# Index scores in tiles of their own, first queries one gate later, three gate projections moved behind the attention's output projection

## The chip, the cores and the metric

The kernel runs on one core of one Trainium2 chip. The metric is the device time of one execution in microseconds (us), as the median of several executions. TensorE (PE), VectorE (DVE), ScalarE (ACT), GpSimd (POOL) and the DMA queues run beside each other and meet through semaphores. TensorE's clock has two levels, 1.2 and 2.4 GHz; the profile shows the granted share as 0.50 and 1.00.

## The reference, cut to what matters

The model is one hybrid block (a convolution branch and a sparse attention branch side by side, then a feed-forward layer) followed by two more layers (gated linear attention and block attention, each with a feed-forward layer). The change lies in the first block alone. There are 272 tokens (16 meta tokens and 256 of the input), 1024 channels, 8 heads of 128 with 2 key groups.

```
proj = h @ w_in                      # u_conv, q, k, v, q_idx, k_idx, w_idx, gates
y_a = conv branch(u_conv)            # a * sigmoid(gate), 31-tap depthwise convolution, layer norm, silu, @ conv_pw_out
dots  = q_idx . k_idx / 8            # 8 index heads
score = sum_h w_idx[h] * relu(dots[h]) / sqrt(8)
keep the 68 best keys of each query (the 16 meta tokens always), softmax attention over them
y_b = attention(...) @ w_o
g_a, g_b = sigmoid(gates)            # 1024 columns each
stream = stream + (g_a * y_a + g_b * y_b) @ w_merge_out
```

## The kernel before, in words

**Weights.** All large weights lie in one DRAM array in the order of their use, cut into halves of 128 x 1024 numbers; one DMA of 1024 KB on SP's queue brings two. Every half is split into two parts for TensorE: ACT copies it into `whi` (line 134), and DVE subtracts that copy from it into `wlo` (line 136). One projection of 128 output rows takes one half and 24 matmuls (8 slices of the contraction, three products each; `proj_tile`, lines 175 to 177). The splits run at most five halves ahead of the projection that stands at the same place of the program (`may_split`, `LOOK` = 5; six buffers each of `whi` and `wlo`). Halves are counted here from 0: 0 to 15 are the convolution's input, 16 to 19 the index queries, 20 and 21 the keys, 22 and 23 the values, 24 to 31 the queries, 32 to 47 the gates, 48 to 55 the attention's output projection, 56 to 63 the convolution's output projection.

**Order.** The order of the instructions on every engine is fixed when the program is built. Among the instructions whose inputs are ready by the builder's estimate, the one that stands first in the program goes first; what stands in a `high_priority` block goes ahead of all that does not. Each engine then runs its own list strictly in order.

**PSUM.** Projections write into `ps_acc` tiles, of which there are four; index scores, transposes and attention use `ps_wk` tiles, four as well. A fifth `ps_acc` projection waits until the first of the four has been read.

**The stages around the change, in the order of the program.**

- Index queries, then the two key projections. After each of them, and after each of the three value projections, a generator `index_scores` (line 467) is moved on by one piece. For each of two query tiles t and each of 8 heads it makes a matmul (line 474), a relu by ACT into a small tile `r` (line 477; its tag `s1` has two buffers and is shared with `rope`) and a multiply-add by DVE (line 478). Then DVE picks the best keys with seven rounds of `max` and `match_replace` (lines 485 and 488).
- Eight query projections, each with `rope` (lines 520 to 524).
- The loop over 8 heads (line 607). Head i has two gate projections, j = 0 for the convolution's gate g_a and j = 1 for the attention's gate g_b, each evacuated by an ACT tanh (line 611), with pieces of the previous head's attention between them. `attend` has scores (line 553), softmax on DVE and ACT (lines 534 to 539), transposes (556 to 561) and, every fourth head, the product with the values (566 to 570) that writes `oT`. `attend_first` treats the two meta queries that the output needs; its first piece (the copy at line 578 and the matmuls at line 580) stands ahead of the first gate.
- `conv()` (line 620). Its 31 taps stand here in the program, but they become ready long before: DVE and ACT take them whenever nothing that stands earlier is ready. DVE's taps are line 389; ACT's products are line 406, added by DVE at line 412 or by an accumulating DMA of POOL's queue (line 410) into `ysum`, which line 423 adds at the end.
- The convolution's layer norm and silu (lines 641 to 660), a `high_priority` block. It needs the whole convolution. DVE adds (645, 646), PE takes the mean (648), DVE subtracts it (650) and sums squares (654), PE and POOL make the reciprocal root (631, 635, 638), then come DVE (658), ACT's silu (659) and the split into `sT` (200 and 202).
- The attention's output projection (line 661): eight projections m0 to m7 over `oT`; DVE evacuates each (line 664) into the gate tile `tg[1]`.
- The convolution's output projection (line 667): eight projections over `sT`; DVE evacuates each (671) with the gate tile `tg[0]`.

Of the kernel before, what the change touches and what calls it, by code (L numbers as in the profile page):

```python
# [65 lines left out]
    FIRST += [(0, 1, 0, 3 * (_k - 5) + _i) for _i in range(3) if _k > 4 and 3 * (_k - 5) + _i < KT]  # L66
FIRST += [(1, 1, 0, _k) for _k in range(KT)]
PACE = 2
LATER = mybir.DependencyInfo(mybir.DependencyClass.NoSync, mybir.DependencyReason.DATA)
LK = 5  # L70
CONV_ACT = (((0,), (1,), 2), ((0,), (1,), 3))
# [13 lines left out]
def tile_hybrid(ctx: ExitStack, tc: tile.TileContext, x, meta, wts, misc, vec, cst, rows, gkw, ng, pos,  # L85
# [13 lines left out]
    def ps_wk():  # L99
        return wk.tile([P, 512], F32, name="ps_wk", tag="ps_wk")  # L100

    def dump(name, ap):
        if dbg and name in dbg:
            nc.sync.dma_start(dbg[name], ap)
# [320 lines left out]
    def rope(o, ps, a, b, ti, parts=()):  # L425
        n = b - a
        sw = sc.tile([P, L], F32, name="sw", tag="s1", bufs=2)[:, :n]
        t1 = sc.tile([P, L], F32, name="t1", tag="s2", bufs=3)[:, :n]
        A.activation(sw[0:64], ps[64:128], AF.Copy)
        A.activation(sw[64:128], ps[0:64], AF.Copy)  # L430
        V.tensor_mul(t1, ps, tabs[:, ti, a:b])
        V.tensor_mul(sw, sw, tabs[:, ti + 1, a:b])
        V.tensor_add(t1 if parts else o, t1, sw)
        for dst, lo in parts:
            A.activation(dst, t1[lo:lo + 32], AF.Copy)
# [31 lines left out]
    def index_scores():  # L467
        for t in range(2):
            nk = P * (t + 1)
            sco = mp.tile([P, SEQ], F32, name="sco", tag="sco", bufs=2)[:, :nk]  # L470
            vm = vmask[:, SEQ - nk:]
            for h in range(8):
                pd = ps_wk()
                PE.matmul(pd[:, :nk], qi[h // 2][:, t * P:(t + 1) * P], kidx[h % 2][:, :nk],
                          start=True, stop=True)
                r = sc.tile([P, SEQ], F32, name="r", tag="s1", bufs=2)[:, :nk]
                A.activation(r, pd[:, :nk], AF.Relu)
                V.scalar_tensor_tensor(sco, r, wix[:, t, h:h + 1], vm if h == 0 else sco,
                                       op0=OP.mult, op1=OP.add)
                if h == 3:  # L480
                    yield
            m8 = mp.tile([P, 8], F32, name="m8", tag="m8", bufs=2)
            n8 = TOP_X
            while n8 > 0:
                V.max(m8, sco)
                if n8 < 8:
                    V.memset(m8[:, n8:], -GONE)
                V.match_replace(sco, m8, sco, GONE)
                n8 -= 8
            b = mp.tile([P, L], F32, name=f"bias{t}")  # L490
            V.memset(b[:, :META], 0.0)
            V.tensor_scalar(sco, sco, -2.0e38, NEG, op0=OP.is_gt, op1=OP.mult)
            V.tensor_add(b[:, META:META + nk], sco, vm)
            bias.append(b)
            dump(f"bias{t}", b[:, :META + nk])
            yield
# [24 lines left out]
    for h in range(N_HEADS):  # L521
        pq = ps_acc()
        proj_tile(pq[:, :NQ], hT, T0, L)
        rope(qT[:, h, :], pq[:, :NQ], T0, L, 0)
    dump("qT", qT)

    oT = (mp.tile([P, KT, NQ], F32R, name="oT_h", tag="oT_h"),
# [47 lines left out]
    def attend_first():  # L575
        ps = ps_wk()[:8, :2 * META].rearrange("p (g k) -> p g k", g=2)
        q2 = mp.tile([P, 2 * N_HEADS], F32, name="q2")
        V.tensor_copy(q2.rearrange("p (h q) -> p h q", q=2), qT[:, :, 0:2])
        for g in range(2):
            PE.matmul(ps[:, g, :], q2[:, 8 * g:8 * g + 8], kT[g][:, :META], start=True, stop=True)  # L580
        l_ = mp.tile([8, 2, META], F32, name="l2")
        st = mp.tile([8, 2, 2], F32, name="st2")
        V.tensor_add(l_, ps, m2[:, None, :].to_broadcast([8, 2, META]))
        V.tensor_reduce(st[:, :, 0], l_, axis=mybir.AxisListType.X, op=OP.max)
        V.tensor_sub(l_, l_, st[:, :, 0:1].to_broadcast([8, 2, META]))
        A.activation(l_, l_, AF.Exp, scale=scale)
        V.tensor_reduce(st[:, :, 1], l_, axis=mybir.AxisListType.X, op=OP.add)
        V.reciprocal(st[:, :, 0], st[:, :, 1])
        V.tensor_mul(l_, l_, st[:, :, 0:1].to_broadcast([8, 2, META]))
        yield  # L590
        pp = ps_wk()
        for g in range(2):
            PE.transpose(pp[:META, 8 * g:8 * g + 8], l_[:, g, :], ident[:8, :8])
        pT = mp.tile([META, 16], F32, name="pT2")
        A.activation(pT, pp[:META, :16], AF.Copy)
        yield
        po = ps_wk()
        for g in range(2):
            PE.matmul(po[:, 8 * g:8 * g + 8], vt[2][:META, g * P:(g + 1) * P], pT[:, 8 * g:8 * g + 8],
                      start=True, stop=True)  # L600
        split(oT[0][:, :, 0:2], oT[1][:, :, 0:2], po[:, :16].rearrange("p (h q) -> p h q", q=2))
        yield

    tg = [mp.tile([P, KT, NQ], F32, name=f"tg{i}", tag=f"tg{i}") for i in range(2)]
    live = [attend_first()]
    next(live[0])
    for i in range(KT):
        for j in range(2):
            pg = ps_acc()
            proj_tile(pg[:, :NQ], hT, T0, L)  # L610
            A.activation(tg[j][:, i, :], pg[:, :NQ], AF.Tanh, scale=0.5)
            for a in live:
                next(a)
        live = [attend(i, t) for t in range(2)]
        for a in live:
            next(a)
    for _ in range(2):
        for a in live:
            next(a)
# [41 lines left out]
    for m in range(KT):  # L661
        py = ps_acc()
        proj_tile(py[:, :NQ], oT, 0, NQ)
        V.scalar_tensor_tensor(tg[1][:, m, :], tg[1][:, m, :], 1.0, py[:, :NQ], op0=OP.add, op1=OP.mult)

    mT = (mp.tile([P, KT, NQ], F32R, name="mT_h", tag="oT_h"), mp.tile([P, KT, NQ], F32R, name="mT_l", tag="oT_l"))
    for m in range(KT):
# [563 lines left out]
def _pack(a):  # L1231
    w = a["w_in"][0]
    c = np.cumsum([0, 2048, 1024, 256, 256, 512, 64, 8, 2048])
    u, q, k, v, qi, ki, wi, g = (w[:, c[i]:c[i + 1]] for i in range(8))
    u, g = _ws(u), _ws(g)
    qi = qi.reshape(D, 4, 2, 2, 32).transpose(0, 1, 3, 2, 4).reshape(D, 512)
    v = v.reshape(2, 4, P, 256).transpose(0, 2, 1, 3).reshape(2, P, HALF)
    pair = lambda z: z.reshape(2, 8, P, HALF).transpose(1, 0, 2, 3).reshape(16, P, HALF)
    gl = a["gla_w_in_2"][0]
    gq, gk, gv, gg, glow = np.split(gl, [512, 1024, 2048, 3072], axis=1)  # L1240
    gu, gd = a["ffn_w_gu_2"], a["ffn_w_down_2"]

    def out_ffn(o, up, down, ahead=()):
        o = o.reshape(KT, P, HALF)
        return o[:4], _first(up), o[4:], _ffn(up, down, True, ahead)

    mw = _xs(a["moba_w_in_2"][0])

    parts = [pair(u), _ws(qi), _ws(k), v, _ws(q), pair(g), _ws(a["attn_w_o"][0]), _ws(a["conv_pw_out"][0]),
             _ws(a["w_merge_out"][0]), _ffn(a["ffn_up"][0], a["ffn_down"][0], False),  # L1250
             _xs(gq), _xs(gv), _xs(gk), _xs(gg), *out_ffn(a["gla_w_out_2"][0], gu[0], gd[0], mw[:4]),
             mw[4:], *out_ffn(a["moba_w_out_2"][0], gu[1], gd[1])]
    wts = np.concatenate(parts)
    wts = np.ascontiguousarray(wts.reshape(-1, 2, P, HALF).transpose(0, 2, 1, 3)).reshape(-1, P, CHUNK)
    k1, k2 = ki[:, :32], ki[:, 32:]
    pad = np.zeros((D, 32), w.dtype)
    m = np.concatenate([k1, wi, pad[:, 8:], k2, pad, glow], axis=1)
    misc = m.reshape(KT, P, NMISC).transpose(1, 0, 2).reshape(P, KT * NMISC)
    col = lambda z: z.reshape(-1, P).T
    taps = lambda z: z.reshape(z.shape[0], -1, P).transpose(2, 1, 0).reshape(P, -1)  # L1260
    vec = np.concatenate([col(a["mix_norm_g"]), col(a["conv_ln_g"]), col(a["conv_ln_b"]), taps(a["conv_dw_w"][0]),
                          col(a["conv_dw_b"]), col(a["ffn_norm_g"]), taps(a["ffn_dw_w"][0]),
                          col(a["ffn_dw_b"])], axis=1)
    rows = [a["final_norm_g"]]
    for i in range(2):
        for j in range(2):
            rows += [a["ln_g_2"][i, j], a["ln_b_2"][i, j]]
    gkw = np.concatenate([a["gla_w_gk_2"][0], a["gla_b_gk_2"]], axis=0)
    return {"x": a["x"], "meta": a["meta_tokens"], "wts": wts, "misc": misc, "vec": vec, "cst": _constants(),
            "rows": np.stack(rows), "gkw": gkw, "ng": a["gla_norm_g_2"], "pos": a["positions_2"]}  # L1270
# [48 lines left out]
```

## Time and profile before

| | us |
|---|---|
| runs shown: median of 3 (lowest to highest) | 1074.39 (1074.29 to 1075.55) |
| the profiled execution, its own time | 1076.28 |
| its span from the first to the last instruction | 1074.5 |
| granted TensorE clock, mean of the span | 0.995 |

The profile is of one execution, which took 1.9 us more than the median of the runs shown; 1.8 us of its time lie outside its span. Busy times are unions of an engine's instructions. A matmul's end is modelled, so a busy PE is not a PE at its peak; waits are read from start times. "Idle before" names what ended an engine's idle time.

### The profile page before, as it was taken

What the parts mean: (1) busy time and instruction counts of PE and PEld (TensorE: products, weight loads), DVE (VectorE), ACT (ScalarE), POOL (GpSimd) and SP (SyncE); (2) the same over time, 40 slices, a digit from 0 to 9 for tenths busy, and PEclk for the clock granted to TensorE, in tenths of its full rate; (3) what the DMA queues carried; (4) which work ended last, traced back from release to release, by engine and by line L of the source; (5) the groups of instructions that cost most, each with busy time, mean ns of one, the idle gap of its engine ahead of it and who ended that gap; (6) DMA issues with size and microseconds to landing.
All of it is one profiled execution on the core that took longest, in us unless ns stands there. A gap on an engine that the chain in (4) does not pass through costs nothing. (4 is left out here: it accounts for less than half of the span.)

```text
span 1074.5 us, 17515 instructions
## 1 busy us (share of the span) xinstructions
PE 1054.8 (98%) x6989; PEld 954.5 (89%) x6989; DVE 739.5 (69%) x1291; ACT 601.0 (56%) x1051; POOL 44.1 (4%) x52
## 2 busy tenths in 40 slices
PE   8999999999999999999999999999999999999997
PEld 8998998899899999977877999999888878999995
DVE  6899999995776767774577655556674766555555
ACT  6897698564555555567463444446256925444440
POOL 0131002100000000000000000000000000000000
PEclk8999999999999999999999999999999999999999
DMA  8886556564354555454453655557263436555541
GB/s 307 246 201 161 191 166 178 148 220 169 142 197 160 195 182 192 174 185 139 153 202 112 236 196 179 180 191 274 79 215 138 164 131 226 187 195 194 173 144 40
DMA packets 33333, 192.37 MB, mean 179 GB/s; under 512 B 3889, under 2 KB 7857, under 8 KB 12002
## 3 DMA queue, kind: packets, MB, share of 16 engines
q1 hardware_dynamic: 28002, 185.02, 49.7%
q0 software_dynamic: 5248, 6.23, 3.6%
q8 instruction: 55, 0.90, 0.3%
q14 instruction: 28, 0.23, 0.1%
HBM read 183.96 MB, written 1.05 MB: 172 GB/s over the span
## 5 line engine op out<-in xcount | busy, mean ns | idle before, releaser
L136 DVE TENSOR_TENSOR wlo<-wraw,whi 128x1024 fp32r<-128x1024 f32 x320 | 388.5, 1223 | 204.8 <-ACT whi L134 203.9
L134 ACT ACTIVATE whi<-wraw 128x1024 fp32r<-128x1024 f32 x322 | 337.3, 1058 | 302.0 <-PE ps_wk L176 117.7
L176 PE MATMUL ps_wk<-hT_l,whi 128*128 128x256 f32 (+1 forms) x976 | 274.9, 282 | 0.0
L177 PE MATMUL ps_wk<-hT_h,wlo 128*128 128x256 f32 (+1 forms) x976 | 274.6, 281 | 0.0
L175 PE MATMUL ps_wk<-hT_h,whi 128*128 128x256 f32 (+1 forms) x976 | 274.2, 281 | 0.0
L175 PEld LDWEIGHTS ps_wk<-hT_h,whi 128*128 128x128 f32 x976 | 184.4, 189 | 1.1
L176 PEld LDWEIGHTS ps_wk<-hT_l,whi 128*128 128x128 f32 x976 | 184.0, 189 | 1.4
L177 PEld LDWEIGHTS ps_wk<-hT_h,wlo 128*128 128x128 f32 x976 | 184.8, 189 | 0.4
L181 PE MATMUL ps_acc<-whi,rg_h 128*128 128x512 f32 x328 | 131.1, 400 | 0.0
L182 PE MATMUL ps_acc<-wlo,rg_h 128*128 128x512 f32 x328 | 129.6, 395 | 0.0
L183 PE MATMUL ps_acc<-whi,rg_l 128*128 128x512 f32 x328 | 127.1, 395 | 0.0
L175 PE MATMUL ps_acc<-hT_h,whi 128*128 128x258 f32 (+2 forms) x352 | 101.9, 290 | 0.0
L177 PE MATMUL ps_acc<-hT_h,wlo 128*128 128x258 f32 (+2 forms) x352 | 100.7, 286 | 0.0
L176 PE MATMUL ps_acc<-hT_l,whi 128*128 128x258 f32 (+2 forms) x352 | 100.5, 285 | 0.0
L183 PEld LDWEIGHTS ps_acc<-whi,rg_l 128*128 128x128 f32 x328 | 61.6, 188 | 14.7 <-DVE rg_l L202 0.2
L181 PEld LDWEIGHTS ps_acc<-whi,rg_h 128*128 128x128 f32 x328 | 61.6, 188 | 14.1 <-ACT rg_h L200 0.2
L182 PEld LDWEIGHTS ps_acc<-wlo,rg_h 128*128 128x128 f32 x328 | 61.7, 188 | 12.8
L181 PE MATMUL ps_acc<-whi,hT_h 128*128 128x512 f32 (+1 forms) x184 | 71.8, 390 | 0.0
L183 PE MATMUL ps_acc<-whi,hT_l 128*128 128x512 f32 (+1 forms) x184 | 70.8, 385 | 0.0
L182 PE MATMUL ps_acc<-wlo,hT_h 128*128 128x512 f32 (+1 forms) x184 | 70.6, 384 | 0.0
L175 PEld LDWEIGHTS ps_acc<-hT_h,whi 128*128 128x128 f32 x352 | 66.2, 188 | 0.3
L176 PEld LDWEIGHTS ps_acc<-hT_l,whi 128*128 128x128 f32 x352 | 66.3, 188 | 0.2
(950 smaller groups left out, 1561.7 us busy)
## 6 DMA issues: line engine op xcount, KB each, us to landing
wraw<-in_wts_dram SPq DMA_DIRECT2D x166, 1024.0 KB, 5.0
ysum<-zs POOLq DMA_DIRECT2D x10, 258.0 KB, 6.9
x<-in_x_dram SPq DMA_DIRECT2D x4, 512.0 KB, 3.8
lg<-in_rows_dram SPq DMA_DIRECT2D x4, 512.0 KB, 3.6
lb<-in_rows_dram SPq DMA_DIRECT2D x4, 512.0 KB, 5.4
wraw<-in_wts_dram SPq DMA_DIRECT2D x2, 512.0 KB, 6.5
out_dram<-x SPq DMA_DIRECT2D x4, 256.0 KB, 2.0
mraw<-in_misc_dram SPq DMA_DIRECT2D x1, 576.0 KB, 12.3
```

What stands on the lines that cost most here:

```text
L134: A.activation(hi, r, AF.Copy)
L136: V.tensor_sub(lo, r, hi.bitcast(F32))
L175: PE.matmul(ps, wh, xh, start=first, stop=False)
L176: PE.matmul(ps, wh, xl, start=False, stop=False)
L177: PE.matmul(ps, wl, xh, start=False, stop=last)
L181: PE.matmul(ps, xh, wh, start=first, stop=False)
L182: PE.matmul(ps, xh, wl, start=False, stop=False)
L183: PE.matmul(ps, xl, wh, start=False, stop=last)
```

## The change

Index scores: the relus of a query tile go into one tile `r8` of eight heads that takes the storage of the gate tile of the same number (`tg0`, `tg1`, free at that time), instead of the two small shared buffers. One PSUM tile takes four heads (query tile 0) or two (query tile 1), and one ACT instruction evacuates it. The generator now has seven pieces instead of five, so that the query projections move it on too. `attend_first` begins behind the first gate instead of ahead of it. The gates j = 0 of heads 5, 6 and 7 leave the head loop and stand behind the attention's output projection, ahead of the convolution's; their weights move to the same place of the weight array. So the halves are now 32 to 44 for the thirteen gates that stay, 45 to 52 for the attention's output projection, 53 to 55 for the three gates that moved; 56 to 63 are what they were.

```diff
+LEFT = 3
...
-            for h in range(8):
-                pd = ps_wk()
-                PE.matmul(pd[:, :nk], qi[h // 2][:, t * P:(t + 1) * P], kidx[h % 2][:, :nk],
-                          start=True, stop=True)
-                r = sc.tile([P, SEQ], F32, name="r", tag="s1", bufs=2)[:, :nk]
-                A.activation(r, pd[:, :nk], AF.Relu)
-                V.scalar_tensor_tensor(sco, r, wix[:, t, h:h + 1], vm if h == 0 else sco,
-                                       op0=OP.mult, op1=OP.add)
-                if h == 3:
+            r8 = mp.tile([P, 8, SEQ], F32, name="r8", tag=f"tg{t}")[:, :, :nk]
+            wide = 512 // nk
+            for h0 in range(0, 8, wide):
+                if h0:
                     yield
+                pd = ps_wk().rearrange("p (a b) -> p a b", a=wide)
+                for a in range(wide):
+                    h = h0 + a
+                    PE.matmul(pd[:, a, :], qi[h // 2][:, t * P:(t + 1) * P], kidx[h % 2][:, :nk],
+                              start=True, stop=True)
+                A.activation(r8[:, h0:h0 + wide, :], pd, AF.Relu)
+                for h in range(h0, h0 + wide):
+                    V.scalar_tensor_tensor(sco, r8[:, h, :], wix[:, t, h:h + 1], vm if h == 0 else sco,
+                                           op0=OP.mult, op1=OP.add)
...
         rope(qT[:, h, :], pq[:, :NQ], T0, L, 0)
+        next(scores, None)
...
-    live = [attend_first()]
-    next(live[0])
+    def gate(j, i):
+        pg = ps_acc()
+        proj_tile(pg[:, :NQ], hT, T0, L)
+        A.activation(tg[j][:, i, :], pg[:, :NQ], AF.Tanh, scale=0.5)
+
+    first = attend_first()
+    live = [first]
     for i in range(KT):
         for j in range(2):
-            pg = ps_acc()
-            proj_tile(pg[:, :NQ], hT, T0, L)
-            A.activation(tg[j][:, i, :], pg[:, :NQ], AF.Tanh, scale=0.5)
+            if j or i < KT - LEFT:
+                gate(j, i)
             for a in live:
-                next(a)
+                next(a, None)
         live = [attend(i, t) for t in range(2)]
         for a in live:
             next(a)
+        if i == 0:
+            live.append(first)
...
         V.scalar_tensor_tensor(tg[1][:, m, :], tg[1][:, m, :], 1.0, py[:, :NQ], op0=OP.add, op1=OP.mult)
+    for i in range(KT - LEFT, KT):
+        gate(0, i)
...
+    g = pair(g)
+    left = [2 * i for i in range(KT - LEFT, KT)]
+    keep = [i for i in range(2 * KT) if i not in left]
...
-    parts = [pair(u), _ws(qi), _ws(k), v, _ws(q), pair(g), _ws(a["attn_w_o"][0]), _ws(a["conv_pw_out"][0]),
+    parts = [pair(u), _ws(qi), _ws(k), v, _ws(q), g[keep], _ws(a["attn_w_o"][0]), g[left], _ws(a["conv_pw_out"][0]),
```

## Rows read from the trace of the kernel before

**Rows 1.** The page's first part, busy time of each engine in the span.

```profile
PE 1054.8 (98%) x6989; PEld 954.5 (89%) x6989; DVE 739.5 (69%) x1291; ACT 601.0 (56%) x1051; POOL 44.1 (4%) x52
```

**Rows 2.** PE's waits: line <- releaser: us in total, times, longest us.

```profile
PE ps_wk L474 <- ACT r L477: 1.8, 2, 1.6
...
PE ps_wk L580 <- DVE q L578: 0.8, 1, 0.8
```

**Rows 3.** Stretches: length, busy us of PE, PEld, DVE, ACT, POOL; clock; DMA.

```profile
136.00:196.70 60.70, 60.59 (x434) 53.40 (x433) 59.85 (x156) 53.45 (x156) 12.62 (x13) 1.00 0.66 170
196.70:224.70 28.00, 25.75 (x207) 24.76 (x206) 25.00 (x53) 18.28 (x33) 1.80 (x1) 1.00 0.43 140
```

**Rows 4.** DVE's timeline about the convolution's end: start us, length us, instruction.

```profile
185.75 1.23 DVE L136 TENSOR_TENSOR wlo<-wraw,whi 128x1024 fp32r<-128x1024 f32 x1
186.88 0.86 DVE L389 SCALAR_TENSOR_TENSOR yc<-hp,dwh,yc 128x248 f32<-128x248 f32 x2
...
196.30 0.46 DVE L389 SCALAR_TENSOR_TENSOR yc<-hp,dwh,yc 128x242 f32<-128x242 f32 x1
...
198.59 1.23 DVE L423 TENSOR_TENSOR yc<-yc,ysum 128x1032 f32<-128x1032 f32 x1 [0.69 <-DMA ysum<-zs]
199.75 1.22 DVE L136 TENSOR_TENSOR wlo<-wraw,whi 128x1024 fp32r<-128x1024 f32 x1
```

**Rows 5.** ACT's timeline, the copy that the split at 199.75 subtracts.

```profile
186.95 1.06 ACT L134 ACTIVATE whi<-wraw 128x1024 fp32r<-128x1024 f32 x1 [0.24 <-PE ps_acc L176]
```

**Rows 6.** DVE's busy time by line 136 alone between 188 and 196.7 us.

```profile
188.00:196.70 8.70, 0.00 (x0) 1.00 0.72 135
```

**Rows 7.** DVE's timeline in the layer norm, output evacuations (L664) among it.

```profile
202.09 0.42 DVE L664 SCALAR_TENSOR_TENSOR tg<-tg,ps_acc 128x258 f32<-128x258 f32 x1
...
204.17 0.42 DVE L664 SCALAR_TENSOR_TENSOR tg<-tg,ps_acc 128x258 f32<-128x258 f32 x1
...
210.46 0.42 DVE L664 SCALAR_TENSOR_TENSOR tg<-tg,ps_acc 128x258 f32<-128x258 f32 x1
...
212.60 0.42 DVE L664 SCALAR_TENSOR_TENSOR tg<-tg,ps_acc 128x258 f32<-128x258 f32 x1
...
213.67 1.20 DVE L136 TENSOR_TENSOR wlo<-wraw,whi 128x1024 fp32r<-128x1024 f32 x1
216.29 2.76 DVE L658 TENSOR_TENSOR yc<-yc,ps_wk 128x258 f32<-128x258 f32 x8 [1.42 <-PE ps_wk L638]
218.97 0.42 DVE L664 SCALAR_TENSOR_TENSOR tg<-tg,ps_acc 128x258 f32<-128x258 f32 x1
...
221.78 0.41 DVE L664 SCALAR_TENSOR_TENSOR tg<-tg,ps_acc 128x258 f32<-128x258 f32 x1
```

**Rows 8.** PE's timeline, from the layer norm to the end of the convolution's output projection.

```profile
203.17 1.14 PE L648 MATMUL ps_wk<-sqb,ones 128*128 128x258 f32 x4 [0.40 <-DVE sqb L646]
203.96 0.47 PE L176 MATMUL ps_acc<-oT_l,whi 128*128 128x258 f32 x1
...
212.86 0.62 PE L631 MATMUL ps_wk<-ones,sqb 128*128 128x1 f32 x6
...
215.68 0.58 PE L638 MATMUL ps_wk<-cs,rs 128*128 128x128 f32 x3 [1.39 <-POOL rs L635]
...
220.12 0.28 PE L175 MATMUL ps_acc<-sT_h,whi 128*128 128x258 f32 x1
...
221.59 0.39 PE L176 MATMUL ps_acc<-sT_l,whi 128*128 128x258 f32 x1 [0.47 <-DVE sT_l L202]
...
243.84 0.28 PE L685 MATMUL ps_acc<-cs,mt_again 128*128 128x2 f32 x2
```

**Rows 9.** Stretches at the program's start and end, columns as in rows 3.

```profile
13.00:19.80 6.80, 6.67 (x27) 6.24 (x28) 6.63 (x12) 5.31 (x10) 0.00 (x0) 0.50 0.78 321
...
1066.80:1071.00 4.20, 0.00 (x0) 0.00 (x0) 4.09 (x8) 0.00 (x0) 0.92 (x1) 1.00 0.00 0
1071.10:1074.50 3.40, 0.00 (x0) 0.00 (x0) 0.20 (x1) 0.00 (x0) 0.00 (x0) 0.50 0.41 154
```

## The prediction, made before the changed kernel ran

> **What bounds the kernel now.** I began with the page's busy times: PE is busy for 98% of the span [rows 1], so a gain can come only from waits of PE, and there are few. Next came PE's waits. The index scores' matmuls wait 1.8 us for ACT's relus, the first queries' matmuls 0.8 us for DVE [rows 2]. Together 2.6 us is what the first two edits can take off PE.
>
> The third view, the stretches, says that this need not reach the end. From 136 to 196.7 us DVE is busy for 59.85 of 60.70 us [rows 3]: DVE and PE are both full there, and DVE's list ends with the convolution, for which the layer norm waits. In the next 28.0 us PE is busy for only 25.75. So the view that matters is DVE's list about 196.7 us. It shows who stands behind whom. The copy for split 53 is done at 188.0 (186.95 + 1.06) [rows 5], yet DVE subtracts it only at 199.75 [rows 4]; between 188 and 196.7 it makes no split at all [rows 6]. Split 52, which stands ahead of `conv()` in the program, came at 185.75; split 53 stands behind it. So DVE takes what stands behind `conv()` only when the taps have run out. The same holds for the evacuations of the output projection (line 664): the first runs at 202.09, and the fifth only at 218.97, behind the layer norm's eight multiplications [rows 7].
>
> **The change part by part.** All times are of the profiled execution (1076.28 us), which is 1.9 us over the median.
>
> *Index scores and first queries.* The wait at line 474 and most of that at line 580 go: up to 2.6 us of PE. DVE's sixteen multiply-adds and the matmuls stay. ACT has six wide relus in place of sixteen. The storage of `r8` is free, and is read out before the first gate writes it. If the waits stay after all, the loss is at most these 2.6 us, and what comes next hides it either way.
>
> *The convolution ends earlier.* The last gate in the head loop is now half 44, so only splits up to 49 stand ahead of `conv()`, where splits up to 52 stood. A split holds DVE for 1.13 us (185.75 to 186.88 [rows 4]). Three fewer make 3.4 us, and DVE has no idle time to lose: the last tap ends at 196.76 - 3.4 = 193.4. Bounds: 0, if something else of DVE's takes the place, and 4.1, if the wait of 0.69 us for the accumulating DMA [rows 4] goes too. I take 3.4, and the whole layer norm moves by as much.
>
> *PE runs out of work sooner.* A projection takes (243.84 - 220.12 - 0.47) / 8 = 2.9 us [rows 8], so three gates are 8.7 us. Before, m3 ended at about 220.12 less four projections (11.6) and the layer norm's pieces behind it (0.62 + 0.58 + 1.39 of wait), that is 205.9 [rows 8]. In the new order three gates less (8.7), no early waits (2.6) and no line 648 ahead of it (1.2, from 0.40 ahead of 203.17 to 203.96) bring its end to 193.4. Then m4 needs a fifth `ps_acc`: it waits for the evacuation of m0, which stands behind the convolution. That one ended at 202.51 and now ends at 199.1. PE stands idle for 5.7 us, and the 2.6 us won early are part of this wait. Split 49 is ready by then.
>
> *The gates that moved are no filler where a wait is.* PE goes on: m4, line 648 (0.8) and m5 until 205.7; m6 waits for the third evacuation (210.88 - 3.4 = 207.5); m6 and m7 with lines 631 and 638 end at about 214 to 215.9. The first gate that moved needs the buffer of m4, so the evacuation that ran at 218.97: it ends at 219.39 - 3.4 = 216.0. The second needs that of m5, 222.19 - 3.4 = 218.8, just in time. Three gates make 216.0 + 8.7 = 224.7, and only then does PE come to the convolution's output projection. Before, it began at 220.12 and lost 0.47 us more, in effect 220.6. By then the layer norm is finished, so that loss goes. **The sum is 224.7 - 220.6 = 4.1 us more**: 1080.4 on the profiled execution, 1078.5 on the median of 1074.39. From there on nothing is changed and PE is the bound, so it reaches the end.
>
> *Costed at nothing.* The tanhs of the three gates now fall among the layer norm's ACT work; ACT is busy for 18.28 of 28.0 us there [rows 3]. The weights are the same loads on SP's queue in another order. The late splits 50 and 51 give their raw buffer back at about 200, and the load that waits for it brings halves used from 224.7 on; with that cover gone it would cost its landing. The gates pass nothing on POOL's queue.
>
> *The clock.* At the start TensorE ran at the lower level, 0.50, from 13.0 to 19.8; at the end, 4.2 us without a matmul passed at 1.00, and then the rows show 0.50 [rows 9]. A wait of 5.7 us is longer than those 4.2. The Trainium skill ("TensorE: Matmul & The Clock Gate", "Why this matters for your kernels") warns of idle gaps between bursts of matmuls, which put the clock back to its lower level; it speaks against this change, and rows 9 agree. By that rule the time would be that of the third rival below rather than 1078.5.
>
> **The rivals.**
>
> *Half of it.* PE does idle until 199.1, but the builder finds gaps for the later evacuations, so that no gate waits. Then PE's work alone counts: 199.1 + 0.8 + 11.6 + 0.62 + 0.58 + 8.7 = 221.4, or 222.8 with the 1.39 at line 638: 0.8 to 2.2 us more than 220.6. For it: DVE has 3.0 us without work between 196.7 and 224.7 [rows 3]. Against it: rows 7 show one thing taken in each gap, and split 213.67 went into the longest. I price it at +1.5, 1075.9.
>
> *Faster.* The evacuations and splits fall among the taps, and PE never runs dry. The place is DVE between m3's end and the last tap; the price is the early waits (2.6) and the 0.47 at `sT_l`, 3.1 us less, 1071.3. It decides at the first evacuation: by the sum of the case above, the change is no loss if that ends before about 197 to 198. For it: taps also wait for ACT's products, and a dry spell would let evacuations in. Against it: rows 6 show 8.7 us without one, and each split among the taps gives back 1.1 of the 3.4 us.
>
> *The clock falls in the wait.* PE comes back at the lower level. For as long as in rows 9 (6.8 us) that costs half of it, 3.4 us; the wait of m6 covers 207.5 - 205.7 = 1.8, so 1.6 remain on top of 4.1: 1080.1. For it: rows 9; against it: no wait of this length lies between matmuls in the trace of before.
>
> *The change doesn't do what it says.* If line 474 still waits, 1.8 us return. In my forecast that is hidden by the wait at m4; in the faster case it leaves a gain of 1.3.
>
> **How the numbers follow.** The forecast has 0.43, the clock 0.20, half of it 0.20, faster 0.17. The forecast's own range is 1077.0 to 1081.5: a convolution that ends 4.1 earlier takes 0.7 off, one that gains 1 us less adds 1, and the part of the clock's price that isn't covered adds 1.6. The range that should hold the time 8 times in 10 is 1072.0 to 1081.5; it leaves out most of the faster case (0.12) and the upper end of the others (0.07). A measurement tells about 0.2%, 2.1 us, from no change. Slower by more: forecast and clock less a little, 0.60. Within it: half of it, and the faster case where line 474 still waits, 0.25. Faster by more: 0.15.
>
> **What would show it.** Right: no PE wait at line 474; the last tap near 193.4; DVE without evacuations until then; PE idle before m4 by some 6 us, released by DVE's line 664; the first gate that moved released by a later one near 216; the convolution's output projection from about 224.7. Wrong: evacuations among the taps, or a convolution that ends no earlier, or a PE that is busy from 190 to 216.

## The result, and the profile after

The changed kernel takes 1089.05 us (median, 1086.55 to 1090.04); the kernel before took 1074.97 beside it. The ratio is 1.0123, 95% interval 1.0107 to 1.0140: slower, as forecast, but by 13.2 us where 4.1 were forecast, and outside the range. (The 13.2 us come from the ratio, as do the differences to the kernel before further down; the two medians lie 14.1 us apart.) The profiled execution took 1089.12 us with a span of 1087.0, 12.5 more than the 1074.5 before.

The first part of the page, busy time of each engine, beside [rows 1]:

```profile
PE 1059.4 (97%) x6989; PEld 959.5 (88%) x6989; DVE 741.0 (68%) x1291; ACT 599.3 (55%) x1041; POOL 44.0 (4%) x52
```

The number of PE's instructions is the same, its busy time 4.6 us longer (1059.4 - 1054.8). The idle time is 1087.0 - 1059.4 = 27.6 us, before 1074.5 - 1054.8 = 19.7. So the loss has two parts: 7.9 us in which PE does nothing, and 4.6 us in which it does the same work more slowly. PE's waits show the first part (columns as in [rows 2]):

```profile
PE ps_acc L176 <- DVE tg L676: 6.9, 2, 4.1
PE ps_wk L586 <- DVE q L584: 3.5, 1, 3.5
```

Line 676 is the evacuation of the output projection (line 664 before), line 586 the first queries (580 before, 0.8 us). The wait at the index scores, 1.8 us before, is gone. Now PE's timeline, beside [rows 8]; lines 660, 643, 650 are 648, 631, 638 of before:

```profile
200.37 0.58 PE L176 MATMUL ps_acc<-oT_h,whi 128*128 128x258 f32 x1 [4.13 <-DVE tg L676]
200.75 0.42 PE L177 MATMUL ps_acc<-oT_l,whi 128*128 128x258 f32 x1
200.96 0.42 PE L178 MATMUL ps_acc<-oT_h,wlo 128*128 128x258 f32 x1
...
201.61 1.92 PE L660 MATMUL ps_wk<-sqb,ones 128*128 128x258 f32 x4
...
209.98 0.58 PE L176 MATMUL ps_acc<-oT_h,whi 128*128 128x258 f32 x1 [2.80 <-DVE tg L676]
...
213.34 0.62 PE L643 MATMUL ps_wk<-ones,sqb 128*128 128x1 f32 x6
...
216.16 0.58 PE L650 MATMUL ps_wk<-cs,rs 128*128 128x128 f32 x3 [1.28 <-POOL rs L647]
...
224.40 0.36 PE L176 MATMUL ps_acc<-hT_h,whi 128*128 128x258 f32 x1
...
233.10 0.28 PE L176 MATMUL ps_acc<-sT_h,whi 128*128 128x258 f32 x1
```

Counted in the trace, 96 matmuls of the output projection (m0 to m3) stand ahead of the first wait and 120 (m0 to m4) ahead of the second: the waits are at m4 and at m5. Look at two things. Behind the wait at 200.37 the matmuls start 0.21 us apart (200.75, 200.96), where at full rate it is 0.12. And line 650, the layer norm's second transpose, runs at 216.16, almost where it ran before (215.68 in [rows 8]); but now 51 matmuls of the output projection and 72 of the gates stand behind it, before 32. So the convolution's output projection starts at 233.10 instead of 220.12. The early part of the order has brought nothing, and the gates are still to be done.

The stretches show the clock (columns: length, busy us of PE, PEld, DVE, ACT, POOL, granted clock, DMA share, GB/s):

```profile
131.40:134.70 3.30, 3.30 (x18) 3.30 (x17) 3.30 (x9) 2.83 (x5) 0.00 (x0) 0.50 0.62 206
196.30:200.30 4.00, 0.00 (x0) 0.00 (x0) 3.90 (x6) 0.92 (x1) 0.00 (x0) 0.92 0.47 131
200.40:206.40 6.00, 6.00 (x24) 5.62 (x25) 4.49 (x11) 1.43 (x4) 0.00 (x0) 0.50 0.51 175
...
210.00:213.30 3.30, 3.30 (x15) 3.30 (x16) 2.07 (x4) 0.00 (x0) 0.00 (x0) 0.50 0.00 0
...
216.80:220.10 3.30, 3.30 (x16) 3.30 (x17) 3.06 (x9) 2.53 (x3) 0.00 (x0) 0.50 0.71 288
```

Four stretches have a granted clock of 0.50, the level of 1.2 GHz, each behind one of the four waits (3.46 us at the first queries, 4.13, 2.80, 1.28). In the kernel before, none of them is there. The two of 3.30 us at the layer norm hold 15 and 16 matmuls, where 27 fit at 0.12 us: some 1.4 us lost in each.

Last, DVE about the convolution's end, beside [rows 4] and [rows 7] (line 390 is the tap, 424 the sum, 662 the layer norm's subtraction):

```profile
192.68 1.23 DVE L390 SCALAR_TENSOR_TENSOR yc<-hp,dwh,yc 128x243 f32<-128x243 f32 x3
...
196.40 1.23 DVE L424 TENSOR_TENSOR yc<-yc,ysum 128x1032 f32<-128x1032 f32 x1 [1.34 <-DMA ysum<-zs]
...
199.90 0.41 DVE L676 SCALAR_TENSOR_TENSOR tg<-tg,ps_acc 128x258 f32<-128x258 f32 x1
...
203.56 1.43 DVE L662 TENSOR_TENSOR yc<-yc,ps_wk 128x258 f32<-128x258 f32 x4 [1.51 <-PE ps_wk L660]
...
209.51 0.41 DVE L676 SCALAR_TENSOR_TENSOR tg<-tg,ps_acc 128x258 f32<-128x258 f32 x1
...
214.01 0.21 DVE L645 TENSOR_SCALAR st<-ps_wk 128x2 f32<-128x2 f32 x2 [1.94 <-PE ps_wk L643]
```

The taps end at 193.91 and the first evacuation comes at 199.90. The second comes only at 209.51, behind the layer norm's subtractions; before it came ahead of them, at 204.17. Now DVE waits for PE as well, 1.51 us for the mean (line 660) and 1.94 for the variance (line 643): both stand in PE's queue behind matmuls that were waiting for DVE's evacuations. So the two engines wait for each other in turn, while a convolution that ends 2.9 us earlier (193.91 for 196.76) does not end the layer norm earlier. How much of the delay this ring makes is told in part by a run below: with the evacuations first, DVE reads the variance (line 645) at 212.81 instead of 214.01.

### The profile page after: what moved, and what is told of

Read it like the earlier page. It is cut to its first block, busy times and chain, and to the rows that moved or that the text cites. A ratio compares the mean times of both kernels' runs of the same rounds, so it can differ in the third digit from the quotient of the medians.

```text
span 1087.0 us, 17484 instructions
## 1 busy us (share of the span) xinstructions
PE 1059.4 (97%) x6989; PEld 959.5 (88%) x6989; DVE 741.0 (68%) x1291; ACT 599.3 (55%) x1041; POOL 44.0 (4%) x52
## 5 line engine op out<-in xcount | busy, mean ns | idle before, releaser
L182 PEld LDWEIGHTS ps_acc<-whi,rg_h 128*128 128x128 f32 x328 | 61.6, 188 | 14.3 <-ACT rg_h L201 0.6
```

The costliest lines, as they stand in the source:

```text
L182: PE.matmul(ps, xh, wh, start=first, stop=False)
```

## The experiments

In all of them the ratio is to the kernel before, timed on the same chip beside it.

### Which part of the change loses

No gate moved, the two other edits as in the changed kernel:

```
-LEFT = 3
+LEFT = 0
```

> The changed kernel with all sixteen gate projections back ahead of the output projection (index scores and first queries stay as changed). Theory (the loss is the three moved gates: without them TensorE runs out of free PSUM tiles while VectorE still has the convolution's taps and splits, and then works at half clock): both waits of 4.13 and 2.80 us at the output projection vanish, the half-clock spells behind them too, and what is left is the index's 1.8 us gained against the longer wait at the first queries (3.5 us for 0.8, and one half-clock spell): 1073.0 to 1077.5 us. Rival (the index tiles and the first queries carry the loss, for instance through VectorE's order): 1085 or more.

Measured: 1078.85 us, 1.0019 (1.0006 to 1.0033), 2.0 us; the median is 1.4 us above the theory's range, and far from the rival's. The two waits at the output projection are gone. The ten executions fall into two groups: three with a mean granted clock of 0.995 took 1075.47 to 1076.34 us, seven with 0.990 to 0.993 took 1078.10 to 1080.11. So most of the 2.0 us goes with the lower clock. The other way round, the kernel before with the three gates moved and nothing else:

```
-            pg = ps_acc()
-            proj_tile(pg[:, :NQ], hT, T0, L)
-            A.activation(tg[j][:, i, :], pg[:, :NQ], AF.Tanh, scale=0.5)
+            if j or i < KT - LEFT:
+                gate(j, i)
...
+    for i in range(KT - LEFT, KT):
+        gate(0, i)
```

> The kernel before with only the three gates moved; index scores and first queries as before. Theory: the two waits and the half-clock spells at the output projection are there as in the changed kernel, the index waits of 1.8 us are back, the 3.5 us wait at the first queries is back at 0.8: 1085 to 1091 us. Rival (the parts of the change only lose together, because the early gain lets TensorE arrive too soon): 1077 to 1080, two thirds of the loss gone.

Measured: 1.0112 (1.0090 to 1.0134), 12.0 us. The waits of both kernels, no gate moved first:

```profile
PE ps_wk L586 <- DVE q L584: 4.1, 1, 4.1
```

```profile
PE ps_acc L176 <- DVE tg L669: 7.9, 2, 5.1
...
PE ps_wk L475 <- ACT r L478: 2.2, 2, 1.6
```

So the gates carry the loss, with the early edits or without. What the index scores and first queries add is a loss of 2.0 us alone, not a gain; beside the gates it is about 1 us, which is not clear of the noise.

### How the loss grows with the gates

One gate moved instead of three (`LEFT = 1`):

> The changed kernel with one gate moved instead of three. Theory (each gate ahead of the output projection fills 2.9 us of wait and clock): TensorE comes 5.8 us later to m4, after the evacuation of m0, so the wait of 4.13 us goes; m5 still waits up to 3 us for that of m1; 75 matmuls stand behind the layer norm's second transpose, against 123 and 32: the convolution's output projection from 224 to 227 us, 1077 to 1082 us. Rival (a step: any moved gate costs the whole since the layer norm splits the order at one place): 1086 or more. Rival (no loss below two gates): under 1077.

Measured: 1082.52 us, 1.0063 (1.0050 to 1.0076), 6.8 us, just above the theory's range. With the 2.0 us of no gate moved, that makes 4.8 us for the first gate and (13.2 - 6.8) / 2 = 3.2 for each of the next two. A gate is 2.9 us of matmuls. The wait at m4 has gone (PE waits 1.38 us for the layer norm's sums at line 660 instead), that at m5 is 2.13 us, and the transposes run at 215.85, where 216.16 and 215.68 stood: the layer norm's end hardly moves, and each gate that is taken out of the time ahead of it is added behind it. No step is seen, and no free first gate.

### Is it the clock, or the waits?

Redundant matmuls, ahead of m3 and of m5, fill the two waits (their result is overwritten by the tile that follows):

```
+FILL = {3: 34, 5: 14}
...
         py = ps_acc()
+        for _ in range(FILL.get(m, 0)):
+            PE.matmul(py[:, :NQ], oT[1][:, KT - 1, 0:P], oT[1][:, KT - 1, :], start=True, stop=True)
         proj_tile(py[:, :NQ], oT, 0, NQ)
```

> The changed kernel with redundant matmuls put where TensorE waits: 34 ahead of the output projection's tile m3 and 14 ahead of m5, each into the tile that is overwritten next, so that the result is the same and only the idle time is filled. Theory (the clock is the greater part of the loss: 13.6 us at half clock behind the waits stretch the output projection and the layer norm's matmuls by some 6.8 us): the granted clock stays at 1.00 from 196 to 220 us and the time falls by 5 to 9 us, to 1080 to 1084. Rival (the waits alone cost, VectorE's chain sets the end, and the clock lies in its shadow): the clock stays up but the time stays within 2 us of the changed kernel's, 1087 to 1091.

Measured: 1086.51 us, 1.0101 (1.0078 to 1.0124), 2.5 us under the changed kernel's median, with intervals that overlap. The stretches of this kernel:

```profile
196.00:200.00 4.00, 4.00 (x34) 3.81 (x32) 2.36 (x3) 0.00 (x0) 0.00 (x0) 1.00 0.39 81
200.00:202.20 2.20, 0.02 (x1) 0.00 (x0) 2.20 (x6) 0.00 (x0) 0.00 (x0) 1.00 0.24 97
202.20:206.00 3.80, 3.78 (x15) 3.41 (x16) 2.75 (x6) 0.80 (x1) 0.00 (x0) 0.55 0.41 121
206.00:216.00 10.00, 8.03 (x66) 7.56 (x64) 8.16 (x19) 5.18 (x12) 1.78 (x1) 1.00 0.35 128
216.10:230.00 13.90, 13.90 (x115) 13.71 (x116) 12.88 (x26) 11.75 (x23) 0.00 (x0) 1.00 0.51 177
```

From 206 us on the clock stays at 1.00, so 210 to 213.3 and 216.8 to 220.1 are cured; one slow stretch is left, behind a wait of 2.20 us for the layer norm's mean, which is new because the last accumulating DMA landed later (the sum that waits for it began at 197.64, not at 196.40). Neither expectation held: the fall lies between them. The transposes stay at 216.06 and the convolution's output projection starts at 230.87. With the clock up behind 216, the 119 matmuls that stand there still take 14.3 us (119 x 0.12), where the kernel before has 32. So the clock is the smaller part, though this run, with its new wait and one slow stretch left, does not give its exact share.

### Two more PSUM tiles

```
-        py = ps_acc()
+        py = ps_wk() if m in (4, 5) else ps_acc()
```

> The changed kernel with the output projection's tiles m4 and m5 in two tiles of the other PSUM pool, so that they need no evacuation. Theory (the wait is for a free PSUM tile): the 4.13 us wait at m4 goes or falls under 1.5, TensorE is at m6 by 202.5, a shorter wait comes at m7 or at the first moved gate, and fewer half-clock spells are left: 1079 to 1086 us. Rival (VectorE's order is the limit, each further tile only moves the wait): within 2 us of the changed kernel, 1087 to 1091.

Measured: 1.0128 (1.0109 to 1.0148), as the changed kernel. The edit did not do what it was for. The builder put the two tiles in the other pool last:

```profile
217.02 0.58 PE L176 MATMUL ps_wk<-oT_h,whi 128*128 128x258 f32 x1
```

so PE still came to a fifth `ps_acc` first, and waited 4.14 us for the same evacuation. This says nothing for or against either theory; it says that an edit to storage is also an edit to the order.

### The evacuations first

The changed kernel, with the one line that reads PSUM put ahead of DVE's other work:

```
-        V.scalar_tensor_tensor(tg[1][:, m, :], tg[1][:, m, :], 1.0, py[:, :NQ], op0=OP.add, op1=OP.mult)
+        with tc.high_priority():
+            V.scalar_tensor_tensor(tg[1][:, m, :], tg[1][:, m, :], 1.0, py[:, :NQ], op0=OP.add, op1=OP.mult)
```

> The changed kernel with one thing more: the evacuations of the output projection come ahead of all other work of VectorE (high priority), so they run among the convolution's taps. Theory (TensorE is the bound; its two waits of 4.13 and 2.80 us for an evacuation, the half-clock spells behind them, and the work that therefore still stands behind the layer norm's wait near 216 us make the loss): no wait for an evacuation above 0.5 us, one half-clock spell or none between 196 and 222 us, 51 matmuls of 0.12 us for 123 behind the layer norm's second transpose, the convolution's output projection from 222 to 224 us: 1075 to 1079. Rival (the taps and so the layer norm come later by what the evacuations take on VectorE, and the three gates cost their 8.7 us all the same): 1082 or more.

Measured: 1078.6 us, 1.0032 (1.0021 to 1.0043). Of the loss of 13.2 us, 9.8 are gone ((1.0123 - 1.0032) x 1075), with the same three gates behind the output projection. DVE's timeline shows evacuations (line 677 here) among the taps:

```profile
190.10 0.42 DVE L677 SCALAR_TENSOR_TENSOR tg<-tg,ps_acc 128x258 f32<-128x258 f32 x1
190.44 1.23 DVE L390 SCALAR_TENSOR_TENSOR yc<-hp,dwh,yc 128x245 f32<-128x245 f32 x3
191.60 0.41 DVE L677 SCALAR_TENSOR_TENSOR tg<-tg,ps_acc 128x258 f32<-128x258 f32 x1
```

and PE's stretches show that the clock holds until 213 us:

```profile
196.00:212.90 16.90, 14.70 (x117) 14.02 (x116) 15.61 (x31) 6.60 (x12) 0.00 (x0) 1.00 0.36 106
213.00:216.00 3.00, 3.00 (x14) 2.47 (x14) 1.27 (x3) 0.00 (x0) 1.79 (x1) 0.50 1.02 352
```

No wait for an evacuation is left, 51 matmuls stand behind the transposes, which run at 214.95, and the convolution's output projection starts at 222.22, as expected. Two waits for late splits (`wlo`) are new, 0.70 us at 199.58 and 1.50 us at 211.47, ahead of the slow stretch at 213 us. The price is small: the taps end 0.7 us later (194.64 for 193.91). This is the run that settles the cause of the greater part: who stands behind whom on DVE.

The kernel before with the gates moved and the evacuations first, index scores and first queries as before:

> The kernel before with the three gates moved and the evacuations at high priority; index scores and first queries as before. Theory (the moved gates alone cost nothing if the evacuations don't stand behind the convolution): the index's waits of 1.8 us are back, the first queries' wait is 0.8 us, no half clock at 131 us: 1074 to 1077.5. Rival (the gates cost something by themselves, since 51 matmuls stand behind the layer norm's second transpose for 32): 1079 to 1082.

Measured: 1077.77 us, 1.0018 (1.0009 to 1.0027), 0.3 us above the theory's range: 1.9 us of loss remain. Its waits for late splits are the likely place (2.1 us in all for `wlo`, in two waits), with one slow stretch from 212 to 216 behind them.

No gate moved, evacuations first:

> No gate moved, evacuations of the output projection at high priority, index scores and first queries as changed. Theory (TensorE is the bound, and with all gates ahead it has no wait for evacuations to lose): nothing to win here, the 4.1 us wait at the first queries stays: 1073.5 to 1078. Rival (the evacuations at high priority take out a wait that TensorE still has behind the layer norm, 0.5 to 2 us): below 1073.5.

Measured: 1080.5 us, 1.0045 (1.0033 to 1.0057), worse than without (1.0019), and slower than the theory and the rival both say. With all gates ahead nothing waits for an evacuation, and moving them up only pushes other work back: PE now waits 2.25 us for `sT_l` at 224.09. The same edit wins 9.8 us in one order and loses 2.8 in the other.

### Where the early 2.6 us went

The index scores' tiles alone (no gate moved, first queries at their old place):

> The kernel before with the index scores' tiles alone (first queries at their old place, no gate moved). Theory (VectorE ends the ropes of the queries at 129.9 us whatever TensorE does, since it is busy without a break there; TensorE that waits less at the index only waits more at the first queries, and then at half clock): no gain, 1074 to 1079 us, with a wait of 3 to 6 us at the first queries. Rival (the index's 1.8 us are won, and it is the later place of the first queries that gives them back): 1072 to 1073.5.

Measured: 1077.68 us, 1.0020 (1.0010 to 1.0030), 2.1 us slower, within the theory's range. The wait at the first queries:

```profile
PE ps_wk L586 <- DVE q L584: 4.5, 1, 4.5
```

DVE's stretches from 85 to 130 us (length, DVE's busy us, clock, DMA), of the kernel before and then of the changed kernel, show what PE comes to there:

```profile
85.00:100.00 15.00, 15.00 (x44) 1.00 0.75 194
100.00:115.00 15.00, 15.00 (x51) 1.00 0.26 77
115.00:130.00 15.00, 15.00 (x32) 1.00 0.67 221
```

```profile
85.00:100.00 15.00, 15.00 (x47) 1.00 0.69 190
100.00:115.00 15.00, 15.00 (x42) 1.00 0.41 140
115.00:130.00 15.00, 15.00 (x36) 1.00 0.44 146
```

DVE has not one free moment there in either kernel. Its copy of the first queries runs at 129.80 before and at 129.92 after. PE that waits less at the index only comes earlier to a result that DVE has at the same time.

But a full DVE is not yet a DVE that can't be earlier. Of its 45 us some 7 are convolution work, for which nothing in this stage waits (the same columns, instructions on `yc` alone; before, then after):

```profile
85.00:130.00 45.00, 7.41 (x15) 1.00 0.56 164
```

```profile
85.00:130.00 45.00, 6.67 (x15) 1.00 0.52 159
```

What changed is the order. Of the generator's pieces six do work now, where four did. So the choice of the best keys of query tile 1 stands in the program behind the first query projection, where it stood behind the second value projection. Its last instruction comes 6.3 us later than before, among the ropes:

```profile
115.68 0.42 DVE L493 TENSOR_TENSOR bias<-sco,cs 128x256 f32<-128x256 f32 x1
```

```profile
122.02 0.41 DVE L498 TENSOR_TENSOR bias<-sco,cs 128x256 f32<-128x256 f32 x1
```

No run tests whether ropes that go ahead of this choice and of the taps would have kept the gain.

Then the first queries were put two gates later still, without and with the moved gates:

```
-    live = [first]
+    live = []
...
-        if i == 0:
+        if i < 2:
             live.append(first)
```

> No gate moved, evacuations at their old priority, index scores as changed, and the first queries two gates (5.8 us) later still than in the changed kernel. Theory (what is left of the loss without the moved gates, 2 us, is the 4.1 us wait at the first queries and the half clock behind it, because VectorE ends the queries' ropes at about 129.9 us whatever TensorE does): no wait there, no half clock at 131 to 136 us, and the index's 1.8 us are kept: 1071.5 to 1074.5 us. Rival (VectorE sets the end of this stage too, so the wait only moves to the layer norm): 1075 to 1078.

> The changed kernel, three gates moved, with the evacuations of the output projection at high priority and the first queries two gates later still. Theory: both losses are gone, at the output projection (as in the run with evacuations first, 1078.6) and at the first queries (3.2 us of wait and some 1.5 us of half clock): 1071.5 to 1075.5. Rival (the gain ahead of the output projection is given back behind it, since VectorE's splits are late there and the layer norm ends no sooner): 1077 to 1080.

> As the run with both cures, but with one gate moved instead of three. Theory: 32 matmuls stand behind the layer norm's second transpose as in the kernel before, VectorE's evacuations are ahead of it, no wait at the first queries: 1071 to 1075, and within 1.5 us of the run with three. Rival (fewer gates behind means more TensorE work ahead and a later layer norm): slower than with three by over 2 us.

Measured: 1.0008 (0.9998 to 1.0019) with no gate moved; 1.0028 (1.0017 to 1.0040) with three and the evacuations first; 1.0000 (0.9989 to 1.0011) with one and the evacuations first. The wait at the first queries falls to 0.5 us, but in all three kernels this row stands in its place, the next matmuls that need the work of DVE and ACT, the first softmax's transposes:

```profile
PE ps_wk L562 <- ACT p__1556 L545: 3.3, 1, 3.3
```

with a slow stretch behind it. The first two times are those of the rivals, though the wait moved to another place than they named; in the third the theory was too low by 0.9 us, one gate is 3.4 us better than three where it allowed 1.5, and its rival, which had three ahead, fell. None of the three beats the kernel before; the last is level with it.

To see whether DVE's full queue returns the gain, twelve of its convolution instructions were left out (in the first half, those of taps 1 to 6, two each), in the kernel before and in the one with the index tiles alone:

```
                 if n % mod not in lanes[j]:
+                    if i0 == 0 and n <= 6:
+                        continue
```

> The kernel before with the first twelve of VectorE's convolution instructions left out (six taps of the first half, 12 x 0.46 = 5.5 us), so that VectorE is not full ahead of the queries' ropes. Output not the reference's: those taps are missing. Theory (VectorE, full from 85 to 130 us, sets when the queries are ready): the ropes end some 5 us earlier, the 0.8 us wait at the first queries goes, the index's waits of 1.8 us stay, the convolution ends earlier and the layer norm's waits shrink: 1071 to 1074.5. It is the base for the next run.

> Index scores' tiles alone, with the same twelve convolution instructions left out as in the run before (output again without those taps). Theory (the index change wins its 1.8 us once VectorE has room): no wait at the index, a wait of under 1 us at the first queries, no half clock there: 1.0 to 2.0 us faster than the run before. Rival (the index tiles cost as much as they win, whatever VectorE does): within 0.5 us of the run before, or slower.

Measured: 1076.36 us, 1.0009 (0.9996 to 1.0021), and 1076.76 us, 1.0009 (0.9998 to 1.0020): no difference between the two, and the first is 1.9 us above its range. But the edit did not make the room that it was to make. In the second kernel the builder drew later taps forward, DVE is busy for 15.00 of 15.00 us in all three stretches again, and the first queries still wait 3.5 us, for 4.5:

```profile
PE ps_wk L588 <- DVE q L586: 3.5, 1, 3.5
```

In the first, DVE does have room for a while, but PE waits longer for the index scores, 3.3 us for 1.8, at a lower clock:

```profile
85.00:100.00 15.00, 12.73 (x34) 0.77 0.89 223
```

So the two kernels don't differ in the index's waits alone, and the pair decides nothing. What the index tiles would be worth on a DVE with room stays open. The last run was to give it room without leaving anything out, with three weight splits on GpSimd, on top of the kernel with no gate moved and the first queries two gates later:

```
+ON_POOL = (23, 26, 29)
...
-                V.tensor_sub(lo, r, hi.bitcast(F32))
+                (nc.gpsimd if h in ON_POOL else V).tensor_sub(lo, r, hi.bitcast(F32))
```

> No gate moved, index scores as changed, first queries two gates later, and three of the weight splits between 85 and 130 us moved from VectorE (1.21 us each) to GpSimd. Nothing is left out. Theory (VectorE's full queue is what returns the index's gain): VectorE has 3.6 us more room, the wait of 3.3 us at the first softmax's transposes falls under 1 us, no half clock at 131 to 140 us: 1072 to 1075. Rival (GpSimd's split takes far longer than VectorE's and the weights come late, or VectorE slows beside it): TensorE waits for wlo of GpSimd, 1076 or more.

Measured: 1081.88 us, 1.0057 (1.0043 to 1.0070). The rival was right, in its second form. Two of POOL's three splits, each with the tap of DVE that stands beside it:

```profile
86.13 3.29 POOL L138 TENSOR_TENSOR wlo<-wraw,whi 128x1024 fp32r<-128x1024 f32 x1 [2.91 <-ACT whi L136]
```

```profile
87.09 2.61 DVE L391 SCALAR_TENSOR_TENSOR yc<-hp,dwh,yc 128x249 f32<-128x249 f32 x1
```

```profile
99.66 2.39 POOL L138 TENSOR_TENSOR wlo<-wraw,whi 128x1024 fp32r<-128x1024 f32 x1 [6.74 <-ACT whi L136]
```

```profile
99.69 2.63 DVE L391 SCALAR_TENSOR_TENSOR yc<-hp,dwh,yc 128x245 f32<-128x245 f32 x1
```

The three splits take 2.55, 3.29 and 2.39 us on GpSimd for 1.21 on DVE, and beside each of them one instruction of DVE takes 2.50 to 2.63 us where it is 0.42 to 0.47 elsewhere. So DVE saved 3 x 1.21 = 3.6 us and lost some 6.4. PE waits 3.1 us for DVE to read `ps_acc` (line 433), in two waits that the kernel without this edit does not have, and the wait at the first softmax's transposes is still 3.4 us.

## Why the prediction was right and wrong

**The convolution ends earlier: right.** Forecast 193.4 for the last tap, measured 193.91, with no evacuation among the taps. What failed is "the whole layer norm moves by as much". The second sum waits for the accumulating DMA 1.34 us, not 0.69, so that it starts only 2.2 us earlier (196.40 for 198.59), and by the transposes nothing is left (216.16 for 215.68).

**PE runs out of work sooner: right, with a wrong term.** The end of m3 was forecast at 193.4 and came at 196.24 (200.37 - 4.13). The step took "no early waits (2.6)" as won by PE, to be lost in the wait at m4. It was not kept. The first gate starts 3.6 us earlier than before (121.28 for 124.90), but at the first queries PE waits 3.46 us for 0.79, and the slow stretch at 131 us comes on top: the fifth gate starts 0.6 us later than before (140.46 for 139.85). Nor did the bound hold that these edits lose nothing beyond the waits they were to remove: alone they are 2.0 us slower than the kernel before. The first evacuation ended at 200.31 (forecast 199.1), and PE idled 4.13 us (forecast 5.7).

**"m4, line 648 and m5 until 205.7; m6 waits for the third evacuation": the step that failed.** The forecast kept DVE's order of [rows 7] and moved it by 3.4 us; that puts the second evacuation's end at 204.58 - 3.4 = 201.2. The order on every engine is made anew for the changed program, and the second evacuation fell behind the layer norm's subtractions, to 209.51. So m5 waited, not m6: from 209.98 on three tiles were left, not two from 207.5 on (by which PE's own work in the forecast ended at 215.9, the evacuation of m4 at 216.0). That is 2.5 us for the later release and 2.9 for the further tile. The two slow stretches behind it take 1.4 us each. Together 8.2 of the 8.4 us by which the first moved gate missed its forecast (224.40 for 216.0). The gates themselves took 8.70 us (224.40 to 233.10; forecast 8.7), and the start of the convolution's output projection carried the whole difference to the end: 233.10 - 220.6 = 12.5, the difference of the spans.

**"The clock falls in the wait": the right mechanism, undersized.** The Trainium skill ("TensorE: Matmul & The Clock Gate", "Why this matters for your kernels") was right to speak against the change. The forecast gave it one stretch at the lower level, 3.4 us with 1.8 of that covered; there were four, PE's busy time rose by 4.6 us, and the wait that was to cover it was followed by the next slow stretch. But filling the waits at m4 and m5 with matmuls brought back only some 2.5 us, with one slow stretch left: the clock is not the cause that decides.

**"Half of it" and "Faster": both fell, in an instructive way.** The condition of the faster case, evacuations among the taps, was made true by hand. The loss shrank to 1.0032 and did not turn into a gain. The price of that rival counted 2.6 us of early waits that PE could not keep, and nothing for the late splits and the clock: there PE waits 0.70 and 1.50 us for splits, and two stretches, at 131 and 213 us, are slow.

**What stays open:** what the index tiles would bring where DVE is not full, or where the ropes go ahead of the choice of keys and the taps; and how the 1.9 us that three moved gates cost with the evacuations first are divided between late splits and clock.

## What to carry to other kernels

An engine that is busy for 98% of the span cannot make up lost time: moving its work behind a wait costs the whole of that work unless something fills the hole, so ask first what the engine will do in the hole, and whether the buffers it needs for that are released by the engine it would be waiting for. A forecast must not shift an old timeline on an engine whose order is made anew; the question is which instruction stands behind which in the new order, and a priority on the one line that frees a buffer was worth 9.8 us here. A wait removed ahead of a place where another engine is full (15.00 of 15.00 us) came back here at the next matmul that needs that engine; look at what fills it, for part of it can be work that could wait.

## What the runs showed of the hardware

A short wait can be enough to bring PE's clock down, and the same wait may not. In the kernel before, PE waits 1.39 us at line 638 [rows 8], and the granted clock stays at 1.00 in the next stretches:

```profile
215.00:218.00 3.00, 2.32 (x18) 2.14 (x19) 1.71 (x6) 1.25 (x3) 0.62 (x1) 1.00 0.68 205
218.00:221.00 3.00, 3.00 (x27) 2.91 (x25) 3.00 (x8) 3.00 (x9) 0.00 (x0) 1.00 0.35 147
```

In the kernel with no gate moved the same transposes wait the same 1.39 us, until 218.21, and the next stretch is slow:

```profile
218.30:221.70 3.40, 3.40 (x16) 3.06 (x16) 2.64 (x8) 2.18 (x6) 0.00 (x0) 0.50 0.90 304
```

The Trainium skill ("TensorE: Matmul & The Clock Gate", "Why this matters for your kernels") warns of idle gaps between bursts of matmuls; the rows agree that gaps bring the clock down, but these of 1.39 us are shorter than the gap that the page names, and the length of the gap does not settle it. Other executions of one kernel differ for what may be the same reason: 35 of the kernel before, in one set, lie between 1073.98 and 1079.54 us. The six of them with a mean granted clock of 0.991 to 0.993 took 1076.92 us or more, the twelve with 0.996 took 1076.53 or less. For a forecast of this kernel, then, a wait of PE of this size may cost about 1.4 us more than its length, or nothing more.

The other surprise is GpSimd beside DVE. Not only was a split 2.0 to 2.7 times as long there (2.39 / 1.21 to 3.29 / 1.21), it also held DVE up, and not evenly: each time one instruction of DVE stood until the split was over. The tap at 87.09 ended at 89.70, some 0.27 us behind the split (86.13 + 3.29 = 89.42); the one at 99.69 ended at 102.32, again 0.27 behind it (99.66 + 2.39 = 102.05); the next taps took 0.47 us as ever. The Trainium skill ("GPSIMD Engine Reference", "Specifications") says that GpSimd shares its SBUF interfaces with VectorE and contends with instructions that have two SBUF inputs; a tap has two, and the rows agree; they show a whole wait of one instruction, not a slower pace of all.
